# Full tiles of a gelu-and-multiply kernel computed in steps of five and three rows

## The chip, the cores and the metric

The kernel runs on one core of one Trainium2 chip. The metric is the device time of an execution in microseconds, as the median of several executions. On this one core the granted clock was 1.00; the runs that count as slow are those more than 1.5% above the fastest of the same kernel.

## The reference

```python
def setup_inputs():
    batch, seq, dim = (32, 512, 2048)
    return {'x': np.random.randn(batch, seq, dim).astype(np.float32)}

def reference(x):
    half_dim = x.shape[-1] // 2
    x1, x2 = (x[..., :half_dim].copy(), x[..., half_dim:].copy())
    gelu_x1 = 0.5 * x1 * (1 + erf(x1 / np.sqrt(2)))
    return (gelu_x1 * x2).astype(np.float32)
```

It reads 134.2 MB and writes 67.1 MB, with one activation and one multiplication for each output element.

## The kernel before

The 16384 rows are cut into 16 tiles of 128 partitions x 8 rows. There are two input buffers and two output buffers. Loads go through the sync engine's queue (q1 in the profile), stores through the scalar engine's (q10), except the stores of the last two tiles, which go through q1. Only the first and the last tile are computed in pieces.

```python
    R = 8
    x_t = x_flat.rearrange("(n p r) d -> n p r d", p=P, r=R)
    o_t = out_flat.rearrange("(n p r) d -> n p r d", p=P, r=R)
    ...
    xpool = ctx.enter_context(tc.tile_pool(name="xpool", bufs=2))
    opool = ctx.enter_context(tc.tile_pool(name="opool", bufs=2))
    ...
    ahead = [load(0), load(1)]
    for i in range(n_tiles):
        x_tile = ahead.pop(0)
        o_tile = opool.tile([P, R, half], out.dtype, name="o_tile")
        last = i == n_tiles - 1
        pieces = i == 0 or last
        steps = ((0, 2), (2, 4), (4, 8)) if pieces else ((0, 8),)
        for lo, hi in steps:
            rows = slice(lo, hi)
            tc.keep_in_program_order(
                nc.scalar.activation(
                    out=o_tile[:, rows, :], in_=x_tile[:, rows, :half], func=GELU
                )
            )
            nc.vector.tensor_mul(
                out=o_tile[:, rows, :],
                in0=o_tile[:, rows, :],
                in1=x_tile[:, rows, half:],
            )
            if pieces and hi % 4 == 0:
                store(nc.sync if last else nc.scalar, i, o_tile, slice(hi - 4, hi))
        if not pieces:
            store(nc.sync if i == n_tiles - 2 else nc.scalar, i, o_tile, slice(0, R))
        if i + 2 < n_tiles:
            ahead.append(load(i + 2))
```

The load of tile i + 2 takes the input buffer of tile i, so it is issued when the multiplication of tile i has ended, at the same moment as the store of tile i. Tile i + 2 in turn waits for that store's landing, because it takes the same output buffer.

## Time and profile before

| | before |
|---|---|
| median of 3 runs | 471.01 us (470.97 to 471.08) |
| bytes moved, mean rate | 201.33 MB, 429 GB/s |
| VectorE (DVE), ScalarE (ACT) busy | 30%, 24% |
| one full tile: ACT, DVE | 7.03 us, 8.69 us, one after the other |
| one full tile's bytes | 8.39 MB in, 4.19 MB out |
| period of a full tile | 29.0 us |

From the page's list of transfers: the transfer, the engine that issues it, the count, the size and the median time from issue to landing:

```profile
out_dram<-o_tile ACTq DMA_DIRECT2D x13, 4096.0 KB, 42.2
```

A store of 4.19 MB takes 42 us to land.

### The profile page before, as it was taken

Reading aid. Unit: us, or ns where it says so; the run is one execution under the profiler, and the core shown is the slowest. Engines: PE = TensorE matmul, PEld = TensorE weight load, DVE = VectorE, ACT = ScalarE, POOL = GpSimd, SP = SyncE. Lnnn points to the kernel's source line nnn. Section 1 sums busy time; section 2 is a strip of 40 time slices with the busy share of each in tenths; the row PEclk is TensorE's granted clock in tenths of the full one; section 3 lists DMA queues with packets and bytes.
Section 4 is the critical chain, followed back from the end, with each engine's and each line's share of the span. In section 5 each row is a group of like instructions: output and inputs, shape, how many; then the busy total and the mean of one; then the engine's idle time right before and its main releaser. Section 6 shows DMA issues by size and latency. Waiting matters only on the chain.

```text
span 469.2 us, 182 instructions
## 1 busy us (share of the span) xinstructions
DVE 139.5 (30%) x20; ACT 114.2 (24%) x21; POOL 0.2 (0%) x4
## 2 busy tenths in 40 slices
DVE  0330332407033070330704307042070520605142
ACT  1320505041050410505005050050501405014060
POOL 0000000000000000000000000000000000000000
DMA  8999999999999999999999999999999999999998
GB/s 358 447 447 447 402 400 495 402 402 447 481 413 402 447 402 492 402 422 427 492 402 402 447 481 413 402 447 430 464 402 425 425 492 402 402 447 492 402 402 358
DMA packets 5040, 201.33 MB, mean 429 GB/s; under 512 B 560, under 2 KB 560, under 8 KB 560
## 3 DMA queue, kind: packets, MB, share of 16 engines
q1 hardware_dynamic: 2880, 142.61, 70.4%
q10 hardware_dynamic: 2160, 58.72, 29.1%
HBM read 134.22 MB, written 67.11 MB: 429 GB/s over the span
## 4 chain that ended last, share of the span: by engine, by line
DMA 72%; DVE 14%; ACT 12%; ACTq 0%; SPq 0%; issue 0%
DMA out_dram<-o_tile 62%; DVE o_tile L65 14%; ACT o_tile L61 12%; DMA x_tile<-in_x_dram 10%; ACTq L101 0%; SPq L45 0%
## 5 line engine op out<-in xcount | busy, mean ns | idle before, releaser
L65 DVE TENSOR_TENSOR o_tile<-o_tile,x_tile 128x8192 f32<-128x8192 f32 (+2 forms) x20 | 139.5, 6985 | 321.2 <-ACT o_tile L61 321.2
L61 ACT ACTIVATE o_tile<-x_tile 128x8192 f32<-128x8192 f32 (+2 forms) x20 | 112.9, 5661 | 341.3 <-DMA out_dram<-o_tile 303.6
L61 ACT ACT_TABLE_LOAD x1 | 1.3, 1283 | 0.7 <-PEq L90 0.7
L90 POOL MEMSET const-bfloat16-1.0<- 128x1 bf16 x1 | 0.1, 102 | 0.0
L90 POOL MEMSET const-uint8-127<- 128x1 uint8 x1 | 0.1, 102 | 0.0
L90 POOL MEMSET const-float32-1.0<- 128x1 f32 x1 | 0.1, 99 | 0.0
L90 POOL MEMSET const-float32-0.0<- 128x1 f32 x1 | 0.1, 98 | 0.2 <-issue 0.2
## 6 DMA issues: line engine op xcount, KB each, us to landing
out_dram<-o_tile ACTq DMA_DIRECT2D x13, 4096.0 KB, 42.2
x_tile<-in_x_dram SPq DMA_DIRECT2D x2, 4096.0 KB, 16.7
out_dram<-o_tile ACTq DMA_DIRECT2D x2, 2048.0 KB, 34.4
out_dram<-o_tile SPq DMA_DIRECT2D x1, 4096.0 KB, 22.7
out_dram<-o_tile SPq DMA_DIRECT2D x2, 2048.0 KB, 7.7
x_tile<-in_x_dram SPq DMA_DIRECT2D x15, 42.1
```

The costliest lines, as they stand in the source:

```text
L61: nc.scalar.activation(out=o_tile[:, rows, :], in_=x_tile[:, rows, :half], func=GELU)
L65: nc.vector.tensor_mul(out=o_tile[:, rows, :], in0=o_tile[:, rows, :], in1=x_tile[:, rows, half:],)
L90: nc = _bacc.Bacc("TRN2", target_bir_lowering=False, num_devices=1)
```

## The change

The intent is overlap: VectorE can begin on the first five rows while ScalarE is still busy with the other three, so a full tile is finished sooner, and its store and the next load are issued sooner.

```diff
-        steps = ((0, 2), (2, 4), (4, 8)) if pieces else ((0, 8),)
+        steps = ((0, 2), (2, 4), (4, 8)) if pieces else ((0, 5), (5, 8))
```

## The prediction

> **What bounds the kernel now.** I began with the page, because its busy shares say at once which of the two kinds of work, arithmetic or transfers, is near its limit.
>
> ```profile
> DVE 139.5 (30%) x20; ACT 114.2 (24%) x21; POOL 0.2 (0%) x4
> ...
> q1 hardware_dynamic: 2880, 142.61, 70.4%
> q10 hardware_dynamic: 2160, 58.72, 29.1%
> HBM read 134.22 MB, written 67.11 MB: 429 GB/s over the span
> ```
>
> The vector engine works 30% of the span and the scalar engine 24%. The two transfer queues together keep the 16 DMA engines occupied for 70.4 + 29.1 = 99.5% of it. That sum can hide holes, since packets may overlap in the records, so I asked for the rate over whole periods. Tiles 2 to 13 start their activation every 29 us, and the windows run from one such start to the next:
>
> ```profile
> 71.62:100.61 28.99, 8.69 (x1) 7.03 (x1) 0.00 (x0) 1.00 1.00 434
> 100.61:129.64 29.03, 8.69 (x1) 7.03 (x1) 0.00 (x0) 1.00 1.00 433
> ...
> 216.78:245.80 29.02, 8.69 (x1) 7.03 (x1) 0.00 (x0) 1.00 1.00 434
> ...
> 420.06:449.07 29.01, 8.69 (x1) 7.03 (x1) 0.00 (x0) 1.00 0.96 416
> 449.07:469.20 20.13, 8.92 (x3) 7.21 (x3) 0.00 (x0) 1.00 0.91 391
> ```
>
> The columns are the window, its length, the busy time of DVE, ACT and POOL, the clock, the DMA share and GB/s. A tile is 128 x 8 rows of 8 KB in and 4 KB out: 8.39 + 4.19 = 12.58 MB. At 433 GB/s that is 29.06 us, which is the period. The arithmetic of a tile, 8.69 + 7.03 = 15.72 us, fits in it with 13.3 us to spare even though the two engines work one after the other. So the period is the transfer of one tile's bytes, at a steady rate.
>
> Now the view that says otherwise, the chain that ended last. One link of it, for one tile, reads:
>
> ```profile
> 100.61 7.04 ACT o_tile L61
> 107.65 0.02 issue
> 107.67 8.70 DVE o_tile L65
> 116.38 0.02 issue
> 116.40 42.26 DMA out_dram<-o_tile
> 158.66 0.02 issue
> 158.68 7.04 ACT o_tile L61
> ```
>
> The activation of tile 2 waits until the store of tile 0 has given its output buffer back. Tile 2's own store then takes 42.26 us, and its landing starts tile 4 (there are two output buffers). One link is 58.07 us and covers two tiles. It contains 15.7 us of arithmetic, and the page books 12% of the chain on ACT and 14% on DVE. Whether that arithmetic matters depends on what the 42.26 us are.
>
> They are almost all queueing. Alone, 4.19 MB at 433 GB/s need 9.7 us. The store of tile 14, issued at 435.84, landed 22.7 us later (458.5), and only 9.5 us of that came after 449.05, when the load of tile 15 ahead of it in the same queue had landed. So a DMA's time to landing is mainly what was queued in front of it. When tile 2 issues at 116.40, the load and store issued by tile 1 at 87.41 are still under way: they land around 129.6, when the activation of tile 3 starts. That leaves 129.64 - 116.40 = 13.2 us of transfer in hand at the moment of issue. The same difference at the start of the kernel is 71.62 - 62.86 = 8.8 us for tile 1, the smallest, and 100.61 - 87.41 = 13.2 us for tile 2. The queues are never close to empty between tiles.
>
> **What the Trainium skill says.** "DMA: Bandwidth & Descriptors", section Bandwidth, gives 435 GB/s as the ceiling of the 16 DMA engines' ports; the steady 433 to 434 GB/s in the windows above is at that ceiling. Its section "Queues, rings and completion order" says that each DMA engine takes packets in turn from the queues that have work, in ring order within one queue. The trace fits: a load (8.39 MB on q1) and a store (4.19 MB on q10) issued together land together (medians 42.1 and 42.2 us), as packets of about twice the size taken in turn would give. "VectorE: DVE Perf Modes", section on the TRN2 errata, gives an fp32 tensor-tensor operation (N + 151)/0.96 ns and the scalar engine (224 + N)/1.2 ns. For N = 8192 that is 8691 and 7013 ns; the trace has 8692 and 7029. "Perfetto Trace Analysis", section Optimizing Scalar/DVE Operations, advises breaking up instructions where scalar or vector work causes bubbles on other engines. Here the engine that would have to have bubbles is the DMA, and the windows show none in the steady part.
>
> **The change part by part.** Durations by shape, before:
>
> ```profile
> L65 DVE TENSOR_TENSOR o_tile<-o_tile,x_tile 128x8192 f32<-128x8192 f32 x14 | 121.7, 8692 | 283.5 <-ACT o_tile L61 283.5
> L61 ACT ACTIVATE o_tile<-x_tile 128x8192 f32<-128x8192 f32 x14 | 98.4, 7029 | 302.5 <-DMA out_dram<-o_tile 281.6 <-DMA x_tile<-in_x_dram 20.9
> ...
> L65 DVE TENSOR_TENSOR o_tile<-o_tile,x_tile 128x4096 f32<-128x4096 f32 x2 | 8.9, 4426 | 7.7 <-ACT o_tile L61 7.7
> ...
> L61 ACT ACTIVATE o_tile<-x_tile 128x4096 f32<-128x4096 f32 x2 | 7.2, 3608 | 6.0 <-DMA x_tile<-in_x_dram 6.0
> ```
>
> From 4096 to 8192 elements DVE grows by 4266 ns, so 1.0415 ns an element and 160 ns fixed. ACT grows by 3421 ns, so 0.835 ns an element and 187 ns fixed. In 14 tiles (1 to 14) one pair of instructions becomes two:
> - Five rows, 5120 elements: ACT 187 + 4276 = 4463 ns, DVE 160 + 5332 = 5492 ns.
> - Three rows, 3072 elements: ACT 187 + 2565 = 2752 ns, DVE 160 + 3199 = 3359 ns.
> - Added busy time: 14 x 187 ns = 2.6 us on ACT and 14 x 160 ns = 2.2 us on DVE, each split over 14 tiles. Both engines already idle over 280 us before exactly these instructions, so it costs nothing.
> - Latency of a tile, start of ACT to end of DVE. Before: 7.03 + 0.03 + 8.69 = 15.75 us. After: ACT's five rows 4.46, a handover of 0.03, DVE's five rows 5.49 and three rows 3.36 behind them, 13.34 us. ACT's three rows end at 7.22 us, before DVE asks for them at 9.98. Each full tile is thus finished 2.4 us sooner, and its store, and the load of the tile two further on, are issued 2.4 us sooner. The first tile's two-row steps in this trace already show ACT running on while DVE works on the rows before, so I expect no hidden serialization.
> - Bytes, number of DMAs, their shapes and their order in both queues: unchanged.
>
> What are the 2.4 us worth? At issue there are at least 8.8 us of transfer ahead in the queues, normally 13.2. Afterwards there would be 11.2 and 15.6. Work put sooner behind a line that never runs out leaves the line's end where it is. The landing that starts the next activation depends on the bytes, not on the issue time, so a store takes about 44.7 us to land instead of 42.26, and a link stays at 58.07.
>
> The two ends: tile 0 and the last tile keep their steps of two, two and four rows, so the 12.8 us before the first activation and the work behind the last one stay. At the tail, tile 14 ends at 433.4 instead of 435.8, but its store lies behind tile 15's load, which occupies the queue until about 449. Tile 15's activation waits for the landing of tile 13's store at 449.05, in both kernels. Sum: 0.0 us from the steady part, 0.0 from the start, 0.0 from the tail. 471.01 us stays about 471.0.
>
> **The rivals.**
> First, the chain read literally: 42.26 us is a fixed latency, and the seven links through tiles 1, 3, ... 13 each lose 2.4 us. That is 16.9 us, for 454 us (3.6% faster). For it: 26% of the chain is ACT and DVE. Against it: 201.33 MB at 435 GB/s already take 462.8 us, so 454 is below the floor, and a 4.19 MB store is not 42 us of work.
> Second, a small gain at the tail. The last two windows show 416 and 391 GB/s instead of 433: 29.01 x 17 + 20.13 x 42 is about 1340 us x GB/s, or 3.1 us of full rate. If part of it were waiting for tile 14, up to 2.4 us would come back: 468.6. For it: these are the only periods below 433. Against it: the latency of the last store and the end of the span must lie in there, packets begun before a window are counted outside it, and tile 14's store moved at full rate as soon as tile 15's load had landed.
> Third, a loss: the extra instructions cost (4.8 us if all lay on the path, 475.8), or a deeper queue mixes loads and stores less well. Half a per cent off the rate would be 2.3 us, 473.3. For it: nothing in the trace but that the rate is so near the ceiling that it can only fall. Against it: both queues are full already, so the mix of packets does not change.
>
> **Range and chances.** The three runs before lie within 0.11 us. I take -0.7 us for a trace of the second rival and +0.9 us for a slightly different pairing of packets: 470.3 to 471.9. Two per cent is 9.4 us. Faster by that would need 461.6 us, under the floor of 462.8, so I give it 0.01. Slower by that would need the pipeline to break, such as a serialization that I can't see: 0.015. The rest is 0.975.
>
> **What would show it.** In the changed profile: ACT at about 4.46 and 2.75 us and DVE at 5.49 and 3.36 us, 14 each; issue of a tile's store 13.3 us after its activation starts instead of 15.8; a store's time to landing up from 42.2 to about 44.6 us; periods still 29.0 us at 433 GB/s; and the last tile's activation still starting near 449. It would be wrong if the periods became shorter than 29.0 us (then the queues did run dry), if time to landing stayed at 42 (then it is latency, not queueing), or if ACT's second step waited for DVE.

## The result, and the profile after

| | before | after |
|---|---|---|
| median of 6 runs | 471.02 us (470.97 to 471.08) | 470.89 us (470.77 to 470.97) |
| ratio of fast runs | | 0.9997 (95% interval 0.9984 to 1.001) |

The change makes no measurable difference. A ratio is the mean time of one kernel's fast runs over that of the other's of the same rounds, so it is not quite the ratio of the medians.

The kernel after, groups of instructions with different shapes kept apart (line, engine, operation, shapes, count, then busy us and mean ns, then idle us before them and what ended it):

```profile
L65 DVE TENSOR_TENSOR o_tile<-o_tile,x_tile 128x5120 f32<-128x5120 f32 x14 | 76.9, 5492 | 279.6 <-ACT o_tile L61 279.6
L61 ACT ACTIVATE o_tile<-x_tile 128x5120 f32<-128x5120 f32 x14 | 62.6, 4469 | 300.8 <-DMA out_dram<-o_tile 279.8 <-DMA x_tile<-in_x_dram 21.0
L65 DVE TENSOR_TENSOR o_tile<-o_tile,x_tile 128x3072 f32<-128x3072 f32 x14 | 46.9, 3352 | 0.0
L61 ACT ACTIVATE o_tile<-x_tile 128x3072 f32<-128x3072 f32 x14 | 38.5, 2747 | 0.0
```

The split does what it was meant to do. The second steps of three rows have 0.0 us of idle time before them: neither engine waits inside a tile. The chain that ended last, one link of it (start, duration, what):

```profile
100.48 4.48 ACT o_tile L61
104.96 0.02 issue
104.99 8.77 DVE o_tile L65 x2
113.76 0.02 issue
113.78 44.68 DMA out_dram<-o_tile
158.46 0.02 issue
158.48 4.48 ACT o_tile L61
```

From the start of the activation to the issue of the store are now 113.78 - 100.48 = 13.30 us, against 116.40 - 100.61 = 15.79 before. The 2.5 us saved reappear in the next entry of the chain: the transfer takes 44.68 us instead of 42.26. The link lasts 158.48 - 100.48 = 58.00 us, before 58.07. Where the arithmetic went down by 2.5 us, the wait went up by 2.4. The list of transfers says so for all thirteen:

```profile
out_dram<-o_tile ACTq DMA_DIRECT2D x13, 4096.0 KB, 44.7
```

The stretches from one activation's start to the next, of the kernel after (window, length, busy DVE, ACT and POOL, clock, DMA share, GB/s):

```profile
100.48:129.48 29.00, 8.76 (x2) 7.12 (x2) 0.00 (x0) 1.00 1.00 434
129.48:158.48 29.00, 8.76 (x2) 7.12 (x2) 0.00 (x0) 1.00 1.00 434
...
419.49:448.69 29.20, 8.76 (x2) 7.12 (x2) 0.00 (x0) 1.00 0.95 413
448.69:469.10 20.41, 8.92 (x3) 7.21 (x3) 0.00 (x0) 1.00 0.90 386
```

The period is what 12.58 MB take at 434 GB/s, as before. The last tile started at 448.69 instead of 449.07 and the span ended at 469.1 instead of 469.2 us. That is 0.1 us between single profiles, too little to explain.

### The profile page after: what moved, and what is told of

It reads as the page before. It is cut to its first block, busy times and chain, and to the rows that moved or that the text cites. A ratio compares the mean times of both kernels' runs of the same rounds, so it can differ in the third digit from the quotient of the medians.

```text
span 469.1 us, 210 instructions
## 1 busy us (share of the span) xinstructions
DVE 140.5 (30%) x34; ACT 115.5 (25%) x35; POOL 0.2 (0%) x4
## 4 chain that ended last, share of the span: by engine, by line
DMA 75%; DVE 14%; ACT 8%; ACTq 0%; issue 0%; SPq 0%
DMA out_dram<-o_tile 66%; DVE o_tile L65 14%; DMA x_tile<-in_x_dram 10%; ACT o_tile L61 8%; ACTq L101 0%; SPq L45 0%
## 5 line engine op out<-in xcount | busy, mean ns | idle before, releaser
L65 DVE TENSOR_TENSOR o_tile<-o_tile,x_tile 128x5120 f32<-128x5120 f32 (+3 forms) x34 | 140.5, 4171 | 319.9 <-ACT o_tile L61 319.9
L61 ACT ACTIVATE o_tile<-x_tile 128x5120 f32<-128x5120 f32 (+3 forms) x34 | 114.3, 3407 | 339.6 <-DMA out_dram<-o_tile 301.8
## 6 DMA issues: line engine op xcount, KB each, us to landing
out_dram<-o_tile ACTq DMA_DIRECT2D x13, 4096.0 KB, 44.7
```

Source lines behind the costliest of these rows:

```text
L61: nc.scalar.activation(out=o_tile[:, rows, :], in_=x_tile[:, rows, :half], func=GELU)
L65: nc.vector.tensor_mul(out=o_tile[:, rows, :], in0=o_tile[:, rows, :], in1=x_tile[:, rows, half:],)
```

## The experiments

The theory is that the transfers set the period, and that they have so much queued in front of them when a tile issues that issuing earlier is worth nothing. Its rivals are that the arithmetic in the chain is on the path, that tile 14 costs something at the tail, or that the added instructions cancel a real gain. The first four runs move the time from the start of a tile's activation to its issue ("latency") down and up. The next four ask what happened in one of them, and whether the change's own edit pays where latency matters. Two more expose the arithmetic altogether, and one is a repetition.

**Much less latency: no multiplication in the full tiles**.

```diff
-            nc.vector.tensor_mul(...)
+            if pieces:
+                nc.vector.tensor_mul(...)
```

> The kernel before, with the multiplication left out in tiles 1 to 14 (a wrong result on purpose). A full tile is then finished about 7.05 us after its activation starts instead of 15.75, so stores and loads are issued 8.7 us sooner, three and a half times what the change gives. Theory (transfers never run dry, so sooner is worth nothing): 470.9 us, within 0.4 us of the kernel before; time to landing of a store rises from 42.2 to about 51 us. First rival (the arithmetic in the chain is on the path): seven links lose 8.7 us each, 61 us in all, 410 us. Second rival (tile 14's lateness costs something at the tail): 468 to 470 us.

Measured: 470.53 us (470.42 to 470.77), ratio 0.9985 (0.9972 to 0.9997). Latency is 7.06 us (107.47 - 100.41). From its list of transfers:

```profile
out_dram<-o_tile ACTq DMA_DIRECT2D x13, 4096.0 KB, 50.9
```

Taking 8.7 us off every full tile, three and a half times what the change takes off, moves the median by 0.5 us (471.07 in the same rounds), slightly more than the 0.4 us that I had allowed. The missing arithmetic turned into 8.7 us more of waiting in the queue (50.9 - 42.2). The first rival's 410 us is refuted. About a tenth of a per cent is there to be had by finishing tiles sooner; where that 0.5 us comes from was not tested.

**Many more instructions: eight steps of one row.**

```diff
-        steps = ((0, 2), (2, 4), (4, 8)) if pieces else ((0, 8),)
+        steps = ((0, 2), (2, 4), (4, 8)) if pieces else tuple((r, r + 1) for r in range(8))
```

> The kernel before, with tiles 1 to 14 in eight steps of one row. Latency of a tile about 10.9 us (one ACT step of 1.05 us and eight DVE steps of 1.23 us), busy time plus 14 x 7 x 0.187 = 18 us on ACT and plus 14 x 7 x 0.160 = 16 us on DVE. Theory: 470.9 us within 0.4 us, issue 10.9 us after the tile's activation starts. Third rival (the added instructions cost, and in the change this cancelled a real gain of the shorter latency): the cost grows sevenfold against the change's one extra pair, while the latency falls only twice as far (4.9 us instead of 2.4), so the time would move away from 470.9, by up to 34 us if all of it counted.

Measured: 470.99 us (470.94 to 471.21), ratio 0.9994 (0.9981 to 1.0008). Latency was 10.30 us, a little better than the 10.9 that I expected. Seven times the added instructions cost nothing, so in the change no cost hides a gain.

**More latency: the activation done two and three times.**

```diff
-            tc.keep_in_program_order(nc.scalar.activation(...))
+            for _ in range(1 if pieces else 2):      # act_thrice: 3
+                tc.keep_in_program_order(nc.scalar.activation(...))
```

> The kernel before, with the activation of tiles 1 to 14 done twice (right result): latency of a tile 22.8 us instead of 15.75. Theory: a transfer needs about 2.4 us from issue to the first bytes (the first load took 12.1 us for 4.19 MB, of which 9.7 are bytes), so the margin is 13.2 - 2.4 = 10.8 us in the steady part and 8.8 - 2.4 = 6.4 us at tile 1. The added 7.03 us exceed only the latter, by about 0.7 us: 471.6 us, periods still 29.0 us, time to landing down to about 35 us. First rival: seven links gain 7.03 us each: 520 us.

> The kernel before, with the activation of tiles 1 to 14 done three times (right result): latency 29.8 us, 14.06 more than before. Theory: this is over the margin of 10.8 us, so the queues run dry once in a tile or two; stepping the tiles through (a pair of load and store starts when it is issued plus 2.4 us or when the pair before has ended, and takes 29.05 us) puts the last tile's activation 27 us later: 498 us, with holes in the DMA share just before the issues and a time to landing of about 31 to 34 us. First rival: seven links gain 14.06 us: 569 us. If the margin were much larger than I think: 471.

Measured: 488.46 us (486.17 to 490.15) for two, ratio 1.0365, and 520.54 us for three (514.31 to 519.03 in three fast runs, 522.04 to 524.12 in three slow ones), ratio of the fast runs 1.0958. The six times of act_thrice form one spread, which the 1.5% rule cuts in two, so this ratio is on the low side. Both miss my numbers, 471.6 and 498, though they are far from the first rival's 520 and 569 too.

That the queues run dry is plain in act_thrice. Its tile 1 issued at 76.80:

```profile
64.00:70.00 6.00, 1.92 (x1) 4.04 (x1) 0.00 (x0) 1.00 1.01 437
70.00:76.00 6.00, 6.00 (x1) 0.00 (x0) 0.00 (x0) 1.00 0.02 5
76.00:82.00 6.00, 0.77 (x1) 4.71 (x1) 0.00 (x0) 1.00 0.77 246
```

From 70 to 76 us the rate is 5 GB/s while DVE computes: this is what arithmetic on the path looks like. (The windows count a packet where it starts, so a share can exceed 1.) In act_twice there is no hole of this length. With each packet spread over its recorded time, the 16 engines are busy 64% of the microsecond from 70 to 71 us and 88% of the next, and fully before and after, though at 278 GB/s instead of 434 from 72 to 74 us. Its queues, from the page (packets, MB, share of 16 engines' span):

```profile
q1 hardware_dynamic: 2880, 142.61, 71.0%
q10 hardware_dynamic: 2160, 58.72, 27.9%
```

Multiplied by the spans, q1 is busy 0.710 x 488.3 = 346.7 us instead of 0.704 x 469.2 = 330.3, and q10 136.2 us instead of 136.5. The same transfers on q1 (all loads, and the last stores) took 16.4 us longer, of the 19.1 us by which the two profiled spans differ (488.3 and 469.2). So most of the loss is not idle engines but slow load packets. Not all of them are slow: the median of the 64 KB packets is 2.42 us in both traces, but 419 of 1920 took over 2.6 us in act_twice, and 11 before. The landing records (they are in the traces, though no view of the profile lists them) of the 16 DMA engines add that before, and in the kernel after, the 16 finish each load, and each store up to tile 13's, within 0.5 us of each other; in act_twice they do so until tile 1, and from its transfers on they are 2.9 to 4.3 us apart, until the last two stores. Tile 1 had issued this close to the end of the queue (start, busy, what; the activation's start marks the end of the transfers issued earlier):

```profile
69.90 0.36 ACTq L49 DMA_DIRECT2D out_dram<-o_tile  x1
71.46 7.03 ACT L62 ACTIVATE o_tile<-x_tile 128x8192 f32<-128x8192 f32 x1 [10.32 <-DMA out_dram<-o_tile]
```

It had 1.56 us of transfer in hand, where the kernel before has 8.8.

**Which tile does the harm: tile 1 alone, or all but tile 1, done twice.**

```diff
-            for _ in range(1 if pieces else 2):
+            for _ in range(2 if i == 1 else 1):                 # tile1_twice
+            for _ in range(1 if pieces or i == 1 else 2):       # twice_from_2
```

> The kernel before, with the activation doubled in tile 1 alone. In act_twice tile 1 issued only 1.56 us (71.46 - 69.90) before the queues would have run dry, less than the 2.4 us from issue to first bytes, and from there on the 16 DMA engines finished each transfer 3 to 4 us apart (0.4 us before) and load packets took 5% longer on average. Theory A (one late issue puts the engines out of step and they stay so, which alone costs): about 486 us, load packets slow to the end. Theory B (slow packets need an issue close to the end of the queue in every tile): the 3.3 us lost at tile 1 and little else, 472 to 475 us.

> The kernel before, with the activation doubled in tiles 2 to 14 but not in tile 1. Tile 1 then keeps its 8.8 us of transfer in hand at issue, and every later tile has 13.2 - 7.0 = 6.2 us, more than the 2.4 us from issue to first bytes. Theory A (the late issue of tile 1 was the trigger): 471 us, periods 29.0 us, queues never dry. Theory B (6 to 7 us in hand are too little in themselves): about 484 us, periods near 30.3 us from the start.

Measured for twice_from_2: 471.11, 470.85 and 470.66 us, and one slow run of 484.26; ratio of the fast runs 0.9994 (0.9974 to 1.0014). Tile 2 of it, in the timeline and in two periods:

```profile
94.79 0.36 ACTq L49 DMA_DIRECT2D out_dram<-o_tile  x1
100.90 7.03 ACT L62 ACTIVATE o_tile<-x_tile 128x8192 f32<-128x8192 f32 x1 [14.86 <-DMA out_dram<-o_tile]
```

```profile
100.90:129.90 29.00, 8.69 (x1) 14.06 (x3) 0.00 (x0) 1.00 1.00 434
129.90:158.90 29.00, 8.69 (x1) 14.05 (x2) 0.00 (x0) 1.00 1.00 434
```

It has 100.90 - 94.79 = 6.1 us in hand and runs at full rate. In act_twice the later tiles have 6.1 to 10.4 us in hand and mostly need more than 30 us:

```profile
104.74:133.73 28.99, 8.69 (x1) 14.06 (x3) 0.00 (x0) 1.00 1.01 418
133.73:164.54 30.81, 8.69 (x1) 14.06 (x2) 0.00 (x0) 1.00 1.02 430
164.54:194.60 30.06, 8.69 (x1) 14.06 (x2) 0.00 (x0) 1.00 0.99 407
```

So in this execution, and by their times in two more, 6 us in hand are enough in themselves, and theory B fails as a rule. The fourth execution, 484.26 us, lies where theory B had put it, although tile 1 was not late; it was not profiled. That only a late issue of tile 1 can set off the loss is therefore not shown. For tile1_twice: 474.59 and 474.99 us in the two fast runs (ratio 1.008), 487.72 and 487.9 in two slow ones. Neither theory's single number holds: it is sometimes the one and sometimes the other. Its profile fell on the slow run of 487.72, with the completions 2.6 to 4.7 us apart from tile 1's transfers until the last two stores.

> tile1_twice once more, unchanged, because its four runs fell into two groups (474.6 and 475.0; 487.7 and 487.9) and only a run of the slower group was profiled. Theory A in the form that the late issue of tile 1 throws the engines out of step in some executions and they then stay so: both groups again, near 475 and 488. If the profile falls in the faster group: the 16 completions of each transfer at most 1 us apart, load packets at 2.42 us and periods of 29.0 us after tile 3. Rival (the faster group is out of step too, but a large lead hides it): completions 3 us apart there as well.

Measured: the same two groups, four fast runs at 474.8 to 475.1 us and two slow ones at 484.5 and 486.3. The profile fell on a slow run again (484.49), so what the engines do in a fast one stays unseen. But within this one profile the completions were 2.9 to 4.1 us apart from tile 1's transfers until the last two stores, and yet the periods from 134.27 to 221.27 were 29.0 us each; only from 250.51 on were they 29.9 to 30.7. Being out of step is therefore not by itself slow. In the three profiles in which tile 1 issued 1.6 us before the end of the queue, the engines went out of step there, as theory A says. It does not say when that costs, and other traces show that a late tile 1 is not the whole story. In act_thrice the distance stayed at or below 1.1 us until 172 us and was about 3 us or more only from 204 us on; in one_row_steps, with nothing late, it went from 0.4 to 1.0 us at 217 us and stayed there. That part stays open: the profiles of tile1_twice are of slow runs alone, and nothing is built on them here.

**The change's edit where latency matters.** The same split, put on act_twice and on act_thrice:

```diff
-        steps = ((0, 2), (2, 4), (4, 8)) if pieces else ((0, 8),)
+        steps = ((0, 2), (2, 4), (4, 8)) if pieces else ((0, 5), (5, 8))
```

> act_twice with the change's steps of five and three rows (activation of each step done twice; right result). Latency of a tile 14.45 us for ACT plus the handover and DVE's last three rows, 3.36: 17.8 us instead of 22.8. Issue of tile 1 then comes 71.5 - 47.05 - 17.8 = 6.6 us before the queues end, and 11.2 us in the later tiles: 471 us, against 488.5 of act_twice without the split, so here the change's own edit is worth 3.6%. If the split only helps by its 5 us of latency in seven links, 488.5 - 35 = 453 us, under the floor; if it does not help where arithmetic is on the path, 488.

> act_thrice with the change's steps of five and three rows (right result). Latency 21.65 us for ACT plus 0.02 and 3.36: 25.0 us instead of 29.8. Tile 1 issues at 47.0 + 25.0 = 72.0, 0.5 us after the queues have run dry, so this stays slow, a little above act_twice's 22.8: between 488 and 500 us (492), against 520.5 without the split.

Measured: act_twice_split 470.93 us (470.77 to 470.97), ratio 0.9998, against 1.0365 without the split. act_thrice_split 496.17 us (495.44 to 500.4), ratio 1.0553, against 1.0958. In the first, latency is 17.84 us and tile 1 issues 71.71 - 65.14 = 6.6 us before the queues would end, as expected, so it stays at the floor. The edit that does nothing to the kernel before saves 17.5 us here. It also does not go below 471 us: the transfers stop it there.

**No transfer queued at all: one output buffer.**

```diff
-    opool = ctx.enter_context(tc.tile_pool(name="opool", bufs=2))
+    opool = ctx.enter_context(tc.tile_pool(name="opool", bufs=1))
```

> The kernel before with one output buffer instead of two (right result). A tile's activation must then wait for the landing of the store just before it, which was issued together with the last load in flight, so nothing is left in the queues while a tile is computed. Theory: period = 15.75 us of arithmetic + 2.4 us from issue to first bytes + 29.05 us of transfer = 47.2 us for tiles 1 to 13 from 71.6 us on, 27.9 for tile 14 which has only its store, and about 21 us for the last tile: 734 us (up to 750 if the load packets are as slow as in act_twice). The DMA is then idle for some 18 us in each period.

> one_obuf with the change's steps of five and three rows. Theory: here the 2.42 us that each of the 14 full tiles is finished sooner lie on the path, 14 x 2.42 = 34 us less than one_obuf: 700 us for 734, ratio 0.954, period 44.8 us, time to landing unchanged. If the split were worth nothing for another reason than the full queues (serialized steps, instruction cost), one_obuf and this would be equal.

Measured: 753.86 us (751.81 to 755.21) without and 717.84 us (716.49 to 719.86) with the split, ratios 1.6 and 1.523 to the kernel before; 717.84 / 753.86 = 0.952. A period of one_obuf in two windows, arithmetic and transfer:

```profile
317.65:333.43 15.78, 8.69 (x1) 7.03 (x1) 0.00 (x0) 1.00 0.00 0
333.43:365.76 32.33, 0.00 (x0) 0.00 (x0) 0.00 (x0) 1.00 0.93 389
```

and of one_obuf_split:

```profile
301.14:314.44 13.30, 8.76 (x2) 7.12 (x2) 0.00 (x0) 1.00 0.00 0
314.44:346.93 32.49, 0.00 (x0) 0.00 (x0) 0.00 (x0) 1.00 0.93 387
```

Here nothing moves while a tile is computed, and the split takes 15.78 - 13.30 = 2.48 us off the idle stretch of each of 14 tiles. That is 34.7 us of the 36.0 measured. Time to landing stays the same, 32.33 and 32.49 us, since there is no queue to wait in. My 734 and 700 us were 20 and 18 too low: a transfer that starts from empty queues needs 32.2 us or more instead of the 29.05 + 2.4 that I had allowed, and some took 34.8.

The runs with two output buffers in one view; "in hand" is the time from tile 1's issue to the end of the transfers issued before it:

| kernel | latency of a full tile, us | in hand at tile 1, us | time, us |
|---|---|---|---|
| gelu_only | 7.1 | 17.4 | 470.5 |
| one_row_steps | 10.3 | 14.3 | 471.0 |
| after | 13.3 | 11.1 | 470.9 |
| before | 15.8 | 8.8 | 471.0 |
| act_twice_split | 17.8 | 6.6 | 470.9 |
| twice_from_2 | 22.8 (15.8 in tile 1) | 8.6 (6.1 in tile 2) | 470.7, 470.9, 471.1 (slow: 484.3) |
| tile1_twice | 15.8 (22.8 in tile 1) | 1.6 | 474.6, 475.0 (slow: 487.7, 487.9) |
| tile1_twice_again | the same | 1.7 | 474.8 to 475.1 (slow: 484.5, 486.3) |
| act_twice | 22.8 | 1.6 | 488.5 |
| act_thrice_split | 25.1 | none | 496.2 |
| act_thrice | 29.9 | none | 514.3 to 519.0 (slow: 522.0 to 524.1) |

Down to 6.6 us in hand at tile 1 the fast runs move by no more than 0.5 us, whatever the latency; at 1.7 us and less they are longer. Between these no run was made.

## Why the prediction was right

- **Durations.** 4463, 2752, 5492 and 3359 ns were expected for the four new instructions, 4469, 2747, 5492 and 3352 measured. Issue at 13.3 us: met.
- **No serialization.** The three-row steps had 0.0 us of idle time before them: met.
- **The queue takes up the gain.** Time to landing was expected at about 44.6 us and was 44.7. This step carries the prediction, and gelu_only shows that it is no coincidence: 8.7 us less latency, 8.7 us more waiting. one_obuf_split shows the reverse: without a queue the landing time stays and the time falls by what the split saves.
- **No cost of the added instructions.** one_row_steps: met.
- **Names of the tiles.** The tile that starts at 100.61 is tile 3, not tile 2 as the prediction calls it below its second view: tile 1 starts at 47.07 and tile 2 at 71.62. So the link shown runs from tile 3 to tile 5, and the transfers in front of its issue are those of tile 2. The differences of times, and with them the 13.2 and 8.8 us in hand, stay right.
- **First rival, the chain as a sum of latencies.** Refuted by gelu_only. The chain is a true sequence of events, but its longest entry was a wait that gets longer when the others get shorter.
- **The floor.** The 462.8 us that the prediction sets against this rival are an estimate from the 435 GB/s of "DMA: Bandwidth & Descriptors". The steady periods here reached 434, and no run took less than 470.4 us.
- **Second rival, the tail.** The last tile began 0.4 us earlier, and the span ended 0.1 us earlier. The full 3.1 us that I had reckoned for the two last windows were not to be had: gelu_only, where tile 14 is ready 8.7 us sooner, gained 0.5 us in all.
- **Third rival, a loss in rate.** The steady periods shown kept their 434 GB/s.
- **What was mis-sized, in the experiments and not in the prediction's sum:** the price of a queue that runs dry. I took 2.4 us from a first load and called it the time from issue to the first bytes. A start from empty queues cost 32.3 - 29.0 = 3.3 us, and the first bytes are the smaller part: in one_obuf the first packet begins 0.95 us after the issue at 333.43, but then the rate is only about 295 GB/s for 3 us before it reaches 434 (packets spread over their recorded time). Beyond this, after a late issue at tile 1 many load packets were slow for much of the execution. The kernel before stays clear of this with 8.8 us, the kernel after with 11.1.

## What to carry to other kernels

Time from issue to landing is mostly the queue in front: before shortening what comes ahead of an issue, read how much transfer is still in hand at that moment (the landing of the previous transfer less the issue), and divide the bytes of a period by its length. If the rate is at its ceiling and several microseconds are in hand, overlapping the arithmetic buys margin and no time. The same edit was worth its full saving in one_obuf, where the transfer rate falls to zero during the arithmetic.

## What the Trainium skill lacked or had wrong

- "DMA: Bandwidth & Descriptors", section Bandwidth, says in its note on the three figures that for transfers between HBM and SBUF the HBM side at about 358 GB/s is what binds. With one core running, loads and stores together held 433 to 434 GB/s in the steady periods here, close to that section's other figure, the 435 of the ports. The note lacks the condition that a remark under the same section's table of sizes has: that the 358 is for both cores of a pair streaming.
- "Perfetto Trace Analysis", section Identifying Dependency Chains, does not say that a transfer's entry in a chain contains the queue ahead of it. Here the same 4.19 MB store took a median of 50.9, 47.7, 44.7 and 42.2 us to land as the latency before it grew from 7.1 over 10.3 and 13.3 to 15.8 us, and the total stayed at 470.5 to 471.0 us.
- "DMA: Bandwidth & Descriptors" gives a fixed cost and a first-byte latency for a single DMA, but no page gives the price of letting both queues run dry: 12.58 MB took 32.2 us or more from empty queues (one_obuf) and 29.0 us from full ones.
- No page says that the 16 DMA engines can go out of step and stay so. They finished each transfer within 0.5 us of each other in the kernel before and 2.9 to 4.3 us apart in act_twice from tile 1 until the last two stores, where the packets of q1 took 346.7 us of an engine's time instead of 330.3. What puts them out of step, and why some load packets become slower, stays open.
